# Two-layer decoder trunk: one pass of 512 columns for both words of the tokens in half of the first expert product, with the modulation loads moved to the second product

## The chip, the cores and the metric

The kernel runs on one core of one Trainium2 chip. The metric is the device time of one execution in microseconds (us). Engines are named as in the profile: PE is TensorE (its weight loads are PEld), DVE is VectorE, ACT is ScalarE, POOL is GpSimd, and SP is the queue that issues the DMAs.

## The reference, cut to what matters

Two residual layers work on 256 tokens of 1024 features. Each layer has a mixer (convolution and forgetting attention in layer 0, sparse attention in layer 1) and then an expert mixer, `peer_ffn`, which this change is about:

```python
def chunk(xc):
    q = (xc @ w_q).reshape(-1, PEER_HEADS, 2, half)
    s = jnp.einsum('thpd,pkd->thpk', q, sub_keys)
    sv, si = lax.top_k(s, PEER_TOPK)
    cand = (sv[:, :, 0, :, None] + sv[:, :, 1, None, :])...
    cv, ci = lax.top_k(cand, PEER_TOPK)
    ...
    g = jax.nn.softmax(cv, axis=-1)
    a = jax.nn.gelu(jnp.einsum('td,thkd->thk', xc, ue))
    return jnp.einsum('thk,thkd->td', (g * a), ve)
```

There are 16384 experts, each one row of `peer_u` and one of `peer_v`. Each layer also scales, shifts and gates its input by six vectors that come out of `silu(c) @ ada_w`.

## The kernel before, in words

The experts are not gathered. The kernel multiplies all of `peer_u` with all tokens, block by block of 128 experts (128 blocks, `j`, each one load of 128 x 1024 floats), puts the gelu of the products into `S`, multiplies `S` by the gate of each token and expert (zero for most), and multiplies that with `peer_v`, again 128 loads.

Every float32 operand is written as a sum of two words: `hi`, rounded by ACT (line L83), and `lo`, the rest, which DVE subtracts (L84). A product is three matmuls, hi·hi, hi·lo and lo·hi (`terms`, issued by `contract`, L105). Loaded words rotate through 5 buffers (`raw`), 3 of `hi` and 3 of `lo`. A `raw` buffer comes free when its `lo` is made, and only then does SP issue the load that takes its place.

One call of `peer` goes through these stages:

1. `score` and `choose`: the query product (`pwq`, `psc`) and the search for the best experts on DVE. `choose` is a generator: its pieces are taken two at a time while the first half of the blocks is multiplied.
2. First half of `mm1`: blocks 0 to 63, in pairs, into one PSUM bank (512 columns) for a pair. The stationary operand is a 128 x 128 piece of the expert word, the moving one 256 tokens, with 8 pieces `k` for a block. At its end `weigh` turns the chosen indices (`pT` on PE, then DVE).
3. Second half of `mm1`: 32 steps of `gating` (`pG`) and one pair of blocks each.
4. `mm2`: 64 pairs of `peer_v` blocks into `y`; here the tokens are stationary and 512 columns of the expert word move.

The modulation vectors need 48 loads of `ada_w` for each layer; each is reduced by one DVE instruction (L157), which waits for its load. Those that stage 1 of the program has not done are handed to `peer(0, early, late)`: `early` has 39 entries (38 loads) and `late` 18 loads. Before, 20 of the early ones go beside the pairs from block 24 on in stage 2, and 19 entries beside the first 32 pairs of `mm2`. `beside` issues a load behind one pair and its reduction behind the next. A load takes a `raw` buffer like an expert block.

The order of each engine's instructions is made by a scheduler at build time from the program and is then fixed: every engine, and SP, runs its list in order, and an instruction that waits holds all behind it. PSUM has eight banks; in `peer` they are `a` (2, the products), `b` (2, `pT` and the sums of squares) and `w` (2 double banks, `psc`, `pG`, `y`).

Of the kernel before, what the change touches and what calls it, by code (L numbers as in the profile page):

```python
# [8 lines left out]
F32R = mybir.dt.float32r  # L9
F16 = mybir.dt.float16  # L10
U32 = mybir.dt.uint32
AF = mybir.ActivationFunctionType
ALU = mybir.AluOpType
# [4 lines left out]
P = 128  # L18
D = 1024
KC = 8  # L20
T = 256
# [31 lines left out]
def trunk(ctx: ExitStack, tc: tile.TileContext, xT, c, ada_w, ada_b, norm_g, even_w, even_wf, even_bf,  # L53
# [3 lines left out]
    V, A, G, PE = nc.vector, nc.scalar, nc.gpsimd, nc.tensor  # L57
# [1 line left out]
    cp = ctx.enter_context(tc.tile_pool(name="const", bufs=1))  # L59
    st = ctx.enter_context(tc.tile_pool(name="stream", bufs=2))  # L60
    ps = [None]
    MIX, PEER = dict(a=2, b=3, y=3), dict(a=2, b=2, w=2)

    def banks(sizes):
        if ps[0] is not None:
# [9 lines left out]
    def load(src):  # L75
        t = st.tile([P, D], F32, tag="raw", bufs=RAW, name="raw")
        nc.sync.dma_start(t, src)
        return t

    def split(raw):  # L80
        hi = st.tile([P, D], F32R, tag="hi", bufs=HI, name="hi")
        lo = st.tile([P, D], F32R, tag="lo", bufs=HI, name="lo")
        A.activation(hi, raw, AF.Copy)  # L83
        V.tensor_tensor(lo, raw, hi.bitcast(F32), op=ALU.subtract)  # L84
        return Op(None, hi, lo)
# [3 lines left out]
    def weights(src):  # L89
        w = split(load(src))  # L90
        if meanwhile[0] is not None:
            meanwhile[0]()
        return w

    def bank(tag, name):
        pool, sizes = ps[0]
        return pool.tile([P, 512], F32, tag=tag, bufs=sizes[tag], name=name)

    def wide_bank(name):
# [3 lines left out]
    def contract(dst, pairs, start=True, stop=True, **kw):  # L103
        for n, (a, b) in enumerate(pairs):
            PE.matmul(dst, a, b, start=start and n == 0, stop=stop and n == len(pairs) - 1, **kw)  # L105

    def over_d(w, x, k0=0, k1=KC, order=(0, 1, 2)):

        return [t for k in range(k0, k1)
                for t in map(terms(w.at(lambda a: a[:, k * P:(k + 1) * P]), x.at(lambda a: a[:, k, :])).__getitem__, order)]  # L110


    def exps():

        tc.keep_in_program_order(A.preload_act_table_set("natural_log_exp_and_others"))
# [584 lines left out]

    def peer(l, early, late, after=None):
        pp = tc.alloc_tile_pool(name="peer", bufs=1, reuse_waits="tile")
        hi, lo = (pp.tile([P, KC, T], F32R, name=f"h_{n}") for n in ("hi", "lo"))
        s0 = tc.alloc_tile_pool(name="s0", bufs=1, side="right", reuse_waits="tile")
        S = [s0.tile([P, 64, T], F32, name="S0"), pp.tile([P, 64, T], F32, name="S1")]
        if True:
# [128 lines left out]
            gated = [0]  # L835

            def mm1(j):


                p = bank("a", "pmm1")  # L840
                for s in range(2):
                    contract(p[:, s * T:(s + 1) * T], over_d(weights(peer_u[l, j + s]), h))
                p = p.rearrange("p (a t) -> p a t", a=2)
                s = S[j // 64][:, j % 64:j % 64 + 2]
                n = gated[0]
                if n < T:
                    A.activation(s[:, :, n:], p[:, :, n:], AF.Gelu_apprx_tanh)  # L847
                if n > 0:
                    A.activation(p[:, :, :n], p[:, :, :n], AF.Gelu_apprx_tanh)
                    V.tensor_tensor(s[:, :, :n], s[:, :, :n], p[:, :, :n], op=ALU.mult)  # L850
# [77 lines left out]
            def spread(fs, n):  # L928

                return [fs[len(fs) * i // n:len(fs) * (i + 1) // n] for i in range(n)]  # L930
# [18 lines left out]
            if l == 0:  # L949
                pinned(rows, bass.AP(tensor=bdr.tensor, offset=bdr.offset, ap=[[0, P], [1, 16 * NB]]))  # L950
            start = 24
            lots = spread(early[:20], (64 - start) // 2)
            for j in range(0, 64, 2):
                mm1(j)
                for _ in range(2):
# [6 lines left out]
                gating(64 + 2 * b)  # L962
                mm1(64 + 2 * b)
            exps()
            for b, fs in enumerate(spread(early[20:], 32)):
                mm2(2 * b)
                beside(fs)
            s0.release()
# [140 lines left out]
```

## Time and profile before

| | us |
|---|---|
| median of 3 runs | 1948.03 (1946.95 to 1949.16) |
| profiled execution, its own time | 1949.57 |
| its span, first to last instruction | 1947.5 |
| layer 0: first half of `mm1`, second half with gating | 187.5, 214.7 |
| layer 0: `mm2`, first and second 32 pairs | 181.0, 177.7 |
| layer 1: first half of `mm1`, second half with gating | 188.0, 214.8 |
| layer 1: `mm2`, first and second 32 pairs | 173.9, 174.1 |

The stages are cut at the first instruction of the next one on PE. The same stage stands in both layers, with the `ada_w` loads in layer 0 alone, so that layer 1 shows what a stage takes without them.

### The profile page before, as it was taken

The numbers are of one execution on the slowest core, as the hardware profiler recorded it, in microseconds if no ns is written. First come the engines' busy times: TensorE is split into PE (matmuls) and PEld (weight loads), VectorE is DVE, ScalarE is ACT, GpSimd is POOL, SyncE is SP. The second block draws the span as 40 slices with busy tenths as digits, with TensorE's granted clock in tenths as the row PEclk, the third lists the DMA queues.
The fourth block names the chain that finished last, engine by engine and source line by source line (L and its number), as shares of the span: only waits on it lengthen the run. The fifth ranks groups of instructions, "written<-read, shape, count | busy, mean of one in ns | idle before, by whom it ended". The sixth has DMA issues, their size and how long they took to land.

```text
span 1947.5 us, 33150 instructions
## 1 busy us (share of the span) xinstructions
PE 1888.0 (97%) x12954; PEld 1695.0 (87%) x12954; DVE 1439.3 (74%) x2918; ACT 929.7 (48%) x1359; POOL 3.6 (0%) x13
## 2 busy tenths in 40 slices
PE   4898999999999999999999989999999999999998
PEld 3788999999999877877788679999999998888887
DVE  7776999788998666666656859994888985555554
ACT  4445444444445444444445654454444454444443
POOL 0000000000000000000000000000000000000000
PEclk8899999999999999999989999999999999999999
DMA  8865568854446777877633124655444456655563
GB/s 308 272 217 195 175 210 262 279 165 160 156 154 219 237 242 260 295 240 252 230 116 104 45 93 153 193 185 183 160 159 152 162 190 192 193 195 194 195 195 119
DMA packets 105591, 375.00 MB, mean 193 GB/s; under 512 B 12715, under 2 KB 16860, under 8 KB 104540
## 3 DMA queue, kind: packets, MB, share of 16 engines
q1 hardware_dynamic: 104860, 372.38, 58.0%
q8 instruction: 101, 1.65, 0.4%
q10 hardware_dynamic: 576, 0.52, 0.1%
q14 instruction: 54, 0.44, 0.1%
HBM read 369.16 MB, written 6.31 MB: 193 GB/s over the span
## 4 chain that ended last, share of the span: by engine, by line
PE 51%; issue 41%; DVE 4%; DMA 2%; ACT 1%; SPq 0%; DVEq 0%; POOL 0%; POOLq 0%; ACTq 0%
PE y L105 18%; PE pmm L105 18%; PE po L105 2%; PE pG L105 1%; PE pq L105 1%; PE pcc L105 1%; DVE lo L84 1%; DMA raw<-in_ada_w_dram 1%; PE s L650 1%; PE pv L105 1%; PE pt L354 1%; PE po_att L665 1%; DMA S<-in_keys_dram 1%; PE pm L183 1%; PE pb L105 1%
## 5 line engine op out<-in xcount | busy, mean ns | idle before, releaser
L83 ACT ACTIVATE hi<-raw 128x1024 fp32r<-128x1024 f32 x588 | 620.6, 1056 | 696.1 <-PE pmm L105 409.8
L84 DVE TENSOR_TENSOR lo<-raw,hi 128x1024 fp32r<-128x1024 f32 x588 | 717.1, 1223 | 186.3 <-ACT hi L83 185.9
L105 PE MATMUL pmm<-h_hi,hi 128*128 128x256 f32 x2048 | 584.4, 286 | 0.0
L105 PE MATMUL pmm<-h_lo,hi 128*128 128x256 f32 x2048 | 578.7, 283 | 0.0
L105 PE MATMUL pmm<-h_hi,lo 128*128 128x256 f32 x2048 | 577.9, 283 | 0.1
L105 PE MATMUL y<-lo,h_hi 128*128 128x512 f32 x1024 | 399.8, 390 | 6.5 <-DVE lo L84 6.5
L105 PE MATMUL y<-hi,h_lo 128*128 128x512 f32 x1024 | 398.2, 389 | 0.0
L105 PEld LDWEIGHTS pmm<-h_hi,hi 128*128 128x128 f32 x2048 | 392.5, 192 | 0.2
L105 PEld LDWEIGHTS pmm<-h_lo,hi 128*128 128x128 f32 x2048 | 392.6, 192 | 0.0
L105 PEld LDWEIGHTS pmm<-h_hi,lo 128*128 128x128 f32 x2048 | 391.7, 192 | 0.6 <-DVE lo L84 0.3
L105 PE MATMUL y<-hi,h_hi 128*128 128x512 f32 x1024 | 357.7, 389 | 0.0
L105 PEld LDWEIGHTS y<-lo,h_hi 128*128 128x128 f32 x1024 | 192.2, 188 | 51.1 <-DVE lo L84 11.4
L105 PEld LDWEIGHTS y<-hi,h_hi 128*128 128x128 f32 x1024 | 192.1, 188 | 40.3 <-ACT hi L83 0.4
L105 PEld LDWEIGHTS y<-hi,h_lo 128*128 128x128 f32 x1024 | 192.2, 188 | 39.6
L157 DVE CUSTOM_DVE_ANT_0 raw<-raw,silu 128x1024 f32<-128x1024 f32 x96 | 117.3, 1224 | 131.4 <-DMA raw<-in_ada_w_dram 131.1
L894 ACT ACTIVATE h_hi<-S 128x512 fp32r<-128x512 f32 x128 | 80.7, 632 | 177.9 <-PE y L105 177.7
L895 DVE TENSOR_TENSOR h_lo<-S,h_hi 128x512 fp32r<-128x512 f32 x128 | 88.1, 691 | 60.4 <-ACT h_hi L894 60.4
L870 DVE TENSOR_TENSOR w<-hot 128x1024 f16<-128x1024 f16 x128 | 88.1, 689 | 45.3 <-PE pG L105 45.3
L866 DVE TENSOR_TENSOR hot<-hot,lane 128x1024 f16<-128x1024 f16 x128 | 87.7, 686 | 0.0
L880 DVE TENSOR_TENSOR S<-S,pG 128x512 f32<-128x512 f32 (+31 forms) x126 | 69.3, 550 | 1.7 <-PE pG L105 1.7
L105 PE MATMUL pG<-w,hot 128*128 128x128 f16 x1024 | 68.4, 220 | 0.0
L847 ACT ACTIVATE S<-pmm 128x512 f32<-128x512 f32 (+31 forms) x126 | 59.9, 476 | 0.0
(273 smaller groups left out, 1873.1 us busy)
## 6 DMA issues: line engine op xcount, KB each, us to landing
raw<-in_peer_u_dram SPq DMA_DIRECT2D x256, 512.0 KB, 3.4
raw<-in_peer_v_dram SPq DMA_DIRECT2D x256, 512.0 KB, 3.6
raw<-in_ada_w_dram SPq DMA_DIRECT2D x96, 512.0 KB, 4.7
raw<-in_even_w_dram SPq DMA_DIRECT2D x24, 512.0 KB, 4.5
raw<-in_odd_w_dram SPq DMA_DIRECT2D x20, 512.0 KB, 4.0
raw<-in_w_q_dram SPq DMA_DIRECT2D x16, 512.0 KB, 3.8
raw<-in_even_wo_dram SPq DMA_DIRECT2D x8, 512.0 KB, 3.4
raw<-in_odd_wo_dram SPq DMA_DIRECT2D x8, 512.0 KB, 3.3
```

Source lines behind the costliest of these rows:

```text
L83: A.activation(hi, raw, AF.Copy)
L84: V.tensor_tensor(lo, raw, hi.bitcast(F32), op=ALU.subtract)
L105: PE.matmul(dst, a, b, start=start and n == 0, stop=stop and n == len(pairs) - 1, **kw)
L157: V.tensor_tensor_reduce(out=w, in0=w, in1=silu, op0=ALU.mult, op1=ALU.add, scale=1.0, scalar=0.0, accum_out=mods[:, l, m:m + 1])
L183: PE.matmul(pm[0], mean_d.to_broadcast([P, P]), sq, start=(k == 0), stop=(k == KC - 1))
L354: PE.transpose(pt[:, n * P:(n + 1) * P], p[:, n * P:(n + 1) * P], ident)
L847: A.activation(s[:, :, n:], p[:, :, n:], AF.Gelu_apprx_tanh)
L866: V.tensor_tensor(pairs(x), words(v), pairs(lane[:, None].to_broadcast([P, UNIT, P])), op=ALU.is_equal)
L870: V.tensor_tensor(pairs(x), pairs(o), words(g), op=ALU.mult)
L880: V.tensor_tensor(s[:, :n], s[:, :n], p[:, 64 * f:64 * f + n], op=ALU.mult)
L894: A.activation(x.hi, s, AF.Copy)
L895: V.tensor_tensor(x.lo, s, x.hi.bitcast(F32), op=ALU.subtract)
```

## The change

- For blocks 0 to 63 the two token words stand beside each other (`both`, k by word by token). The hi piece of the expert word streams both, 512 columns, in one matmul; the lo piece streams the hi tokens, 256 columns, into the second half of the same bank. A block has 16 matmuls in place of 24.
- A block now fills a bank: 256 columns of hi·hi and 256 of the two others. ACT copies the second half to `S`, DVE adds the first half to it (a new instruction for each block), and the gelu goes from `S` to `S` for a pair.
- The banks become `a` (4) and `w` (2); what asked for `b` in `peer` now takes an `a`.
- All 39 early entries go beside the first 32 pairs of `mm2`, none beside `mm1`.

```diff
-    MIX, PEER = dict(a=2, b=3, y=3), dict(a=2, b=2, w=2)
+    MIX, PEER = dict(a=2, b=3, y=3), dict(a=4, w=2)
...
     def bank(tag, name):
         pool, sizes = ps[0]
+        tag = tag if tag in sizes else "a"
         return pool.tile([P, 512], F32, tag=tag, bufs=sizes[tag], name=name)
...
-        hi, lo = (pp.tile([P, KC, T], F32R, name=f"h_{n}") for n in ("hi", "lo"))
+        both = pp.tile([P, KC, 2, T], F32R, name="h_both")
+        hi, lo = both[:, :, 0], both[:, :, 1]
...
             def mm1(j):
+                if gated[0] == 0:
+                    t = S[j // 64][:, j % 64:j % 64 + 2]
+                    for s in range(2):
+                        w, p = weights(peer_u[l, j + s]), bank("a", "pmm1")
+                        for k in range(KC):
+                            a, b = (x[:, k * P:(k + 1) * P] for x in (w.hi, w.lo))
+                            PE.matmul(p, a, both[:, k].rearrange("p u t -> p (u t)"), start=(k == 0),
+                                      stop=(k == KC - 1), skip_group_check=True)
+                            PE.matmul(p[:, T:], b, hi[:, k], start=False, stop=(k == KC - 1), skip_group_check=True)
+                        A.activation(t[:, s], p[:, T:], AF.Copy)
+                        V.tensor_tensor(t[:, s], t[:, s], p[:, :T], op=ALU.add)
+                    A.activation(t, t, AF.Gelu_apprx_tanh)
+                    return
                 p = bank("a", "pmm1")
...
-            lots = spread(early[:20], (64 - start) // 2)
+            lots = spread([], (64 - start) // 2)
...
-            for b, fs in enumerate(spread(early[20:], 32)):
+            for b, fs in enumerate(spread(early, 32)):
                 mm2(2 * b)
                 beside(fs)
```

The change moves instructions in two places that matter below. The first is the list of SP in `mm2` of layer 0, from the third pair on; `in_peer_v_dram` is an expert block, `in_ada_w_dram` a modulation load. Before:

```order
L77 DMA raw<-in_peer_v_dram 128x1024 x4
L77 DMA raw<-in_ada_w_dram 128x1024
L77 DMA raw<-in_peer_v_dram 128x1024 x4
L77 DMA raw<-in_ada_w_dram 128x1024
L77 DMA raw<-in_peer_v_dram 128x1024 x2
L77 DMA raw<-in_ada_w_dram 128x1024
L77 DMA raw<-in_peer_v_dram 128x1024 x4
```

The same place of SP's list in the changed kernel:

```order
L77 DMA raw<-in_peer_v_dram 128x1024 x2
L77 DMA raw<-in_ada_w_dram 128x1024
L77 DMA raw<-in_peer_v_dram 128x1024 x2
L77 DMA raw<-in_ada_w_dram 128x1024
L77 DMA raw<-in_peer_v_dram 128x1024 x2
L77 DMA raw<-in_ada_w_dram 128x1024 x2
L77 DMA raw<-in_peer_v_dram 128x1024 x2
```

Before, most modulation loads have four expert blocks between them; over the first 64 blocks the list has 18 of them, and 5 times only two blocks (one pair) stand between two. Now it has 36 over these 64 blocks, 28 times with one pair between two, and 6 times two in a row.

The second place is the list of DVE at the end of the first half of `mm1` in layer 0, where the chosen indices come back from PE in `pT`. `hot`, `gr` and `w` are made for the gates, `lo` for the next blocks. Before:

```order
L828 CAST hot<-pT 128x512 x2
L84 TENSOR_TENSOR lo<-raw,hi 128x1024
L866 TENSOR_TENSOR hot<-hot,lane 128x1024 x2
L830 TENSOR_SCALAR gr<-pT 128x256
L84 TENSOR_TENSOR lo<-raw,hi 128x1024
L831 CAST hot<-gr 128x512
```

In the changed kernel L852 is the new addition, with the number of the bank that it reads:

```order
L84 TENSOR_TENSOR lo<-raw,hi 128x1024
L852 TENSOR_TENSOR S_1600<-S_1600,pmm_3744 128x256
L830 CAST hot<-pT 128x512 x2
L832 TENSOR_SCALAR gr<-pT 128x256
L881 TENSOR_TENSOR hot<-hot,lane 128x1024
L84 TENSOR_TENSOR lo<-raw,hi 128x1024
L852 TENSOR_TENSOR S_1600<-S_1600,pmm_3769 128x256
```

PE's list has the block of `pmm_3769`, then the six transposes into three `pT` banks, then the block of `pmm_3820`. Before, `pT` had banks of its own; now `pmm_3769`, three `pT` and `pmm_3820` take the four `a` banks in turn, and the last of them takes the bank that the addition of `pmm_3769` empties.

## Rows read from the trace of the kernel before

**Rows 1.** The page: span, and busy time, share and instructions of each engine.

```profile
span 1947.5 us, 33150 instructions
PE 1888.0 (97%) x12954; PEld 1695.0 (87%) x12954; DVE 1439.3 (74%) x2918; ACT 929.7 (48%) x1359; POOL 3.6 (0%) x13
```

**Rows 2.** Busy time by stage: `mm1` halves of layers 0 and 1, then `mm2`.

```profile
core 0: us, PE busy (x) PEld busy (x) DVE busy (x) ACT busy (x) POOL busy (x), PEclk, DMA share, GB/s
209.45:396.98 187.53, 187.53 (x1576) 186.98 (x1575) 173.10 (x533) 87.55 (x100) 0.00 (x0) 1.00 0.72 234
1188.49:1376.47 187.98, 187.88 (x1576) 187.07 (x1575) 153.43 (x495) 87.60 (x100) 0.00 (x0) 1.00 0.56 182
396.98:611.66 214.68, 214.68 (x2050) 213.30 (x2049) 190.10 (x283) 100.77 (x162) 0.00 (x0) 1.00 0.49 161
...
611.66:792.61 180.95, 176.65 (x770) 143.41 (x769) 119.53 (x142) 86.60 (x100) 0.00 (x0) 1.00 0.77 257
...
1591.25:1765.19 173.94, 173.94 (x768) 143.99 (x768) 102.31 (x99) 86.30 (x99) 0.00 (x0) 1.00 0.60 196
```

**Rows 3.** The chain that ended last, layer 1: start, length, what, how many.

```profile
1224.96 139.51 PE pmm L105 x1161
...
1377.54 5.80 PE pmm L105 x48
...
1591.25 348.21 PE y L105 x1536
```

**Rows 4.** Busy time in layer 1 until the choice of experts is done.

```profile
1188.49:1303.00 114.51, 114.41 (x964) 113.65 (x963) 113.06 (x449) 54.38 (x62) 0.00 (x0) 1.00 0.57 183
```

**Rows 5.** Waits in that stretch: who waited for whom, total us, times, longest.

```profile
PEld pmm L105 <- DVE lo L84: 0.3, 1, 0.3
```

**Rows 6.** Groups by shape in layer 0's gating: 256 columns read from PSUM.

```profile
L880 DVE TENSOR_TENSOR S<-S,pG 128x256 f32<-128x256 f32 x1 | 0.4, 414 | 0.0
...
L882 ACT ACTIVATE S<-pG 128x256 f32<-128x256 f32 x1 | 0.4, 383 | 0.1
```

**Rows 7.** Timeline of DVE in layer 1, around the return of the chosen indices.

```profile
1364.72 1.29 DVE L828 CAST hot<-pT 128x512 f16<-128x512 f32 x2 [0.90 <-PE pT L826]
1365.93 0.68 DVE L866 TENSOR_TENSOR hot<-hot,lane 128x1024 f16<-128x1024 f16 x1
1366.53 1.22 DVE L84 TENSOR_TENSOR lo<-raw,hi 128x1024 fp32r<-128x1024 f32 x1
1367.66 0.69 DVE L866 TENSOR_TENSOR hot<-hot,lane 128x1024 f16<-128x1024 f16 x1
1368.27 0.42 DVE L830 TENSOR_SCALAR gr<-pT 128x256 f32<-128x256 f32 x1
```

**Rows 8.** Waits from 611 to 790 us, nearly the first 32 pairs.

```profile
DVE raw L157 <- DMA raw<-in_ada_w_dram: 49.2, 17, 4.0
...
PEld y L105 <- DVE lo L84: 7.6, 8, 1.4
```

**Rows 9.** Timeline of DVE there, two modulation loads with one pair between.

```profile
660.98 1.23 DVE L157 CUSTOM_DVE_ANT_0 raw<-raw,silu 128x1024 f32<-128x1024 f32 x1 [2.79 <-DMA raw<-in_ada_w_dram]
...
662.13 1.22 DVE L84 TENSOR_TENSOR lo<-raw,hi 128x1024 fp32r<-128x1024 f32 x1
663.27 0.68 DVE L895 TENSOR_TENSOR h_lo<-S,h_hi 128x512 fp32r<-128x512 f32 x1
663.88 1.22 DVE L84 TENSOR_TENSOR lo<-raw,hi 128x1024 fp32r<-128x1024 f32 x1
667.86 1.23 DVE L157 CUSTOM_DVE_ANT_0 raw<-raw,silu 128x1024 f32<-128x1024 f32 x1 [2.77 <-DMA raw<-in_ada_w_dram]
...
669.01 1.22 DVE L84 TENSOR_TENSOR lo<-raw,hi 128x1024 fp32r<-128x1024 f32 x1
```

**Rows 10.** Timeline of PE at the end of that stretch.

```profile
670.29 0.50 PE L105 MATMUL y<-lo,h_hi 128*128 128x512 f32 x1 [0.69 <-DVE lo L84]
```

**Rows 11.** Timeline of SP there: the issue of the second load.

```profile
663.38 0.33 SPq L77 DMA_DIRECT2D raw<-in_ada_w_dram  x1
```

## The prediction

> **What bounds the kernel now.** Start with the page: PE is busy 1888.0 of 1947.5 us [rows 1], so a gain has to come out of PE's list, and a loss is a gap in it. The table by stage is next, because the two layers run the same expert stages, and only layer 0 has modulation loads in them. In the first half of `mm1` PE has no gap in layer 0 and 0.1 us in layer 1, with the granted clock at 1.00 [rows 2]. In `mm2` the first 32 pairs take 180.95 us in layer 0, with 4.30 us of PE idle, and 173.94 us in layer 1, with none [rows 2]. What differs is the `ada_w` loads: 7.01 us.
>
> The chain gives the pace of PE where it waits for nothing: 139.51 us for 1161 matmuls of 256 columns (120.2 ns each) in `mm1`, 5.80 us for 48 (120.8) between gates, and 348.21 us for 1536 of 512 columns (226.7) in `mm2` [rows 3]. Twice the columns cost 106.5 ns more, and 13.7 ns are left over for each matmul whatever its length. Each has its own weight load.
>
> **PE's part of the change.** For one `k` the old list has three matmuls of 256 columns, 3 x 120.2 = 360.6 ns; the new one has one of 512 and one of 256, 226.7 + 120.2 = 346.9 ns. It streams the same 768 columns and saves the left-over of one matmul, 13.7 ns. There are 64 blocks x 8 = 512 of these in a layer: 7.0 us per layer, 14.0 us in all. Below, nothing is saved if the left-over goes with columns and not with matmuls; more than 14.0 I see no row for.
>
> The Trainium skill, "TensorE: Matmul & The Clock Gate", section "Back-to-back issue gap", gives a gap of N/2.4 + 2.5 ns at full clock, and its Part 2 says that the engine pulls a weight load ahead of running matmuls. By that the saving would be 1024 x 2.5 = 2.6 us. The rows of this case have 13.7 where the page has 2.5, at both lengths, so I go by the rows.
>
> **What the new join costs.** Each block adds on ACT a copy of 128x256 out of PSUM, 383 ns in the nearest row, and on DVE an addition of 128x256 with one operand in PSUM, 414 ns; the gelu stays one instruction for a pair [rows 6]. ACT is busy 87.6 of 188 us there [rows 2]; 64 x 0.38 = 25 us more leaves it slack. DVE has none to spare at first: in layer 1 it is busy 113.06 of the first 114.51 us, until the experts are chosen [rows 4], and it fell so far back that PE once waited for a `lo`, 0.3 us [rows 5]. Over the whole half it is busy 153.43 us [rows 2]; with 64 x 0.41 = 26 us it comes to 180, and the half should shrink to 188.0 - 7.0 = 181. Back to back, an instruction begins before the one ahead has ended (a `lo` of 1.22 us lets the next begin after 1.14 [rows 9]), which leaves a few us. So the sum just fits, and the lists spread the choice over more blocks than before. I take 1.5 us of waiting for late `lo` words in a layer; 0 if the lists keep pace, 7 us if all of PE's gain is lost to DVE.
>
> Layer 0 loses its modulation loads from this half. That gains nothing by itself, since PE did not wait there [rows 2]; it makes the room for the additions on DVE, 19 x 1.23 = 23 us [rows 9] against 26.
>
> **The shared banks.** With `b` gone, the three `pT` take `a` banks, and the next block needs the bank that the addition of `pmm_3769` frees. That addition stands on DVE behind two casts, `gr`, `hot` and a `lo`, all of which begin after `pT`. From the timeline, start to start: two casts 1.21, `hot` 0.60, a `lo` 1.13 [rows 7]; then `gr` and the addition, 0.42 [rows 7] and 0.41 [rows 6]: 3.8 us in which PE has nothing in its list that it may begin. Before, `pT` had banks of its own and PE went on. I take 3.8 us per layer; below 0 if the bank comes free otherwise, above 5 with a wait for the copy on ACT.
>
> Together each layer's first half gains 7.0 - 1.5 - 3.8 = 1.7 us: 3.4 us in all (from a gain of 14 to a loss of 10). The second half of `mm1` keeps its instructions and its 214.7 us [rows 2].
>
> **The moved loads.** What a modulation load does in `mm2` is seen in rows 8 to 11. DVE waits 49.2 us for such loads, 17 times [rows 8]. Why it waits shows in the timeline. DVE reduces a load at 660.98, makes a `lo` at 662.13, which ends at 663.35 and sets a `raw` buffer free; at 663.38 SP issues the next modulation load into it [rows 9, 11]. DVE makes one more `lo` and then stands before the reduction until 667.86, 4.5 us after the issue, with the next `lo` behind it [rows 9]. That one begins at 669.01, and PE, which needs it, goes on at 670.29 after a gap [rows 9, 10]. From reduction to reduction this is 667.86 - 660.98 = 6.88 us, while PE wants a pair in 24 x 0.2267 = 5.44 us. A pair with such a turn around costs 1.44 us, and the next one as much, because the loop feeds itself.
>
> With four blocks between two loads the loop has two pairs of time, 10.9 us, and costs nothing. That fits the whole: five places with one pair between two loads in the old list, and 7.01 us more than layer 1: 1.40 us each. It is a delay and no lack of rate: DMA is 0.77 busy at 257 GB/s [rows 2], and the same engines had 0.72 in `mm1` of layer 0.
>
> The new list has 28 such places over these pairs, and six times two loads in a row. The first two I let the lead of the three `hi` and `lo` buffers absorb: 26 x 1.40 = 36.4 us, less the 7.0 that are there now: 29.4 us more. The second load of a doubled pair is not in any row. Below it is free, as both wait in the same 4.5 us; above it adds a turn of its own and its reduction, 6 x (1.44 + 1.15) = 15.5 us. I take nothing for it. For the whole term: below -7 (if all come in time, as they did in `mm1`, where a pair took 5.8 us and DVE interleaved them with other work), above 29.4 + 15.5 = 45.
>
> **Sum.** -3.4 + 29.4 = +26 us on the span of 1947.5, and as much on the executions: the profiled one took 1949.57 with 2.1 us around its span, the median of the runs is 1948.03. Forecast: 1948.0 + 26 = 1974 us, 1.3% slower.
>
> **Rivals.**
> *The loads hide.* The list puts a reduction behind both `lo` of a pair, and if DVE does other work while the load comes, the loop takes less than 5.44 us and the 29.4 fall away. For it: in `mm1` of layer 0 twelve pairs in a row had a load each, and PE never waited [rows 2]. Against it: those pairs were 5.8 us long and DVE had the choice of experts to do in between; in `mm2` it has 2.9 us of work for a pair and stands still for the rest [rows 9]. Then the time is 1948 - 3.4 - 7 = 1938, or 1931 with the banks free too. It decides below about 0.4 us per such place: 26 x 0.4 = 7.0 + 3.4. Faster.
> *DVE falls behind in `mm1`.* Both halves lose PE's gain and the banks cost 5 us: 14.0 - 2 x (7 + 5) = -10, so 1948 + 10 + 29.4 = 1987. For it, [rows 4, 5]; against it, the sum over the whole half, which fits.
> *The weight load is hidden.* If the left-over does not go with the matmul, PE gains nothing, but DVE keeps pace too: 1948 + 29.4 + 2 x 3.8 = 1985. For it: only that no row has the two lengths in turn; against it, the same 13.7 ns at 256 and 512 columns [rows 3]. The gap of the Trainium skill named above ("TensorE: Matmul & The Clock Gate", "Back-to-back issue gap") would make it 1982.
> *Half the loads hide*, in the first pairs and after each gap: 14 x 1.40 - 7.0 - 3.4 = +9, 1957.
>
> **How the numbers follow.** The forecast has 0.56, DVE falling behind 0.12, the hidden weight load 0.06, half of the loads hiding 0.13, and all of them hiding 0.13. The predicted time is the first case's, 1974. The range of 8 in 10 runs from 1953 (below it the loads that hide and a little of the half case) to 1990 (above it the doubled loads at their full price): about 0.14 and 0.06 are left out. A measurement of this kernel tells 0.2%, 4 us, from no change. Faster than 1944 is the case of hidden loads, 0.11; within 4 us its near side, 0.05; slower holds 0.84.
>
> **What would show it.** In the changed profile: 512-column `pmm` matmuls at 226.7 ns and 256 ones at 120.2; one gap of 3 to 4 us on PE behind `pT` in each layer; first halves of `mm1` at 185 to 187 us; the first 32 pairs of layer 0's `mm2` at 210 us with some 30 us of PE idle ended by `lo`, and DVE waiting for `ada_w` loads some 35 times; the other stages as now. Wrong would be a stretch of `mm2` near 181 us, or `mm1` halves near 181 or above 190, or a granted clock below 1.00 in the stretch with the gaps, which the gaps of now do not show [rows 2].

## The result, and the profile after

The changed kernel takes 1960.07 us (median of 5 runs, 1957.81 to 1961.44), the kernel before 1948.02 (5 runs, 1946.95 to 1949.16). The ratio is 1.0052, with a 95% interval of 1.0039 to 1.0065: 12 us slower, where 26 were forecast. The time lies inside the range.

The page of the changed kernel has the same two rows as [rows 1]. PE has 1024 matmuls fewer and 5 us less to do, on a span that is 12.2 us longer:

```profile
span 1959.7 us, 31492 instructions
PE 1883.0 (96%) x11930; PEld 1638.1 (84%) x11930; DVE 1479.9 (76%) x3046; ACT 967.9 (49%) x1487; POOL 3.6 (0%) x13
```

The table by stage answers to [rows 2]: first halves of `mm1` in layers 0 and 1, then the first 32 pairs of `mm2` in layer 0.

```profile
core 0: us, PE busy (x) PEld busy (x) DVE busy (x) ACT busy (x) POOL busy (x), PEclk, DMA share, GB/s
211.04:395.91 184.87, 184.22 (x1064) 159.35 (x1063) 172.12 (x556) 106.30 (x163) 0.00 (x0) 1.00 0.58 183
...
610.52:810.28 199.76, 183.84 (x770) 144.71 (x769) 138.54 (x179) 86.08 (x99) 0.00 (x0) 0.98 0.83 281
...
1202.59:1388.58 185.99, 184.77 (x1065) 159.40 (x1063) 173.13 (x557) 106.30 (x163) 0.00 (x0) 1.00 0.58 184
```

Stage by stage, cut at the first instruction of each on PE:

| stage | before | after | forecast | measured |
|---|---|---|---|---|
| up to the first `pmm` | 209.45 | 211.04 | 0 | +1.6 |
| first half of `mm1`, layer 0 | 187.53 | 184.87 | -1.7 | -2.7 |
| first half of `mm1`, layer 1 | 187.98 | 185.99 | -1.7 | -2.0 |
| `mm2`, layer 0, first 32 pairs | 180.95 | 199.76 | +29.4 | +18.8 |
| its second 32 pairs, to the first `pkc` | 195.39 | 192.97 | 0 | -2.4 |
| `pkc` to layer 1's first `pmm` | 200.49 | 199.34 | 0 | -1.2 |

The other stages are within 0.1 us. The rows add up to +12.1. The +1.6, -2.4 and -1.2 were not forecast. They lie in code that the diff does not touch; behind `y`, at least, its PE list has another order (`pyT` and the sums of squares stand otherwise between the `pbias` matmuls). From `y` to `pkc` alone the kernels below take 14.0 to 21.7 us, so nothing is built on it.

The waits of the stretch with the loss answer to [rows 8]:

```profile
DVE raw L158 <- DMA raw<-in_ada_w_dram: 53.2, 32, 3.3
...
PEld y L106 <- DVE lo L84: 22.7, 22, 2.7
PE y L106 <- DVE lo L84: 13.6, 11, 2.3
ACT hi L83 <- DMA raw<-in_peer_v_dram: 11.5, 4, 6.6
```

DVE waits 32 times for a modulation load, nearly the 35 of the forecast, but 1.7 us each in place of 2.9. Three pieces of that stretch show how unequal the pairs are: four pairs with one load each, then one pair behind two loads in a row, and the last two pairs.

```profile
696.22:719.11 22.89, 22.85 (x97) 17.71 (x96) 15.61 (x20) 10.59 (x13) 0.00 (x0) 1.00 0.84 275
719.11:728.39 9.28, 7.33 (x25) 5.59 (x24) 7.79 (x10) 2.75 (x4) 0.00 (x0) 0.82 0.84 280
794.02:810.28 16.26, 13.36 (x49) 9.95 (x48) 8.54 (x12) 4.33 (x6) 0.00 (x0) 0.90 0.94 349
```

A single load costs 22.89 / 4 - 5.44 = 0.28 us; the pair behind the doubled one costs 3.84. Half of that is the clock (PE is busy for 7.33 us in place of 5.44): behind a gap of 1.95 us on PE the granted clock is 0.50 from 721.8 to 725.1, the lower of its two levels (1.2 in place of 2.4 GHz), and 0.82 in the mean of the piece, where every stage of [rows 2] has 1.00. A gap of 2.30 us, which ended at 777.21, left it at 1.00.

In the last two pairs, at the turn to the second 32 and 5.4 us over the pace, the constants of the next mixer come through the same queue. The DMA engines are 0.94 busy there, ACT waits 11.4 us for expert words, and DVE stands before the scaling of one of the constants; DVE and then PE:

```profile
801.33 0.15 DVE L528 TENSOR_SCALAR og<-og 128x1 f32<-128x1 f32 x1 [4.80 <-DMA og<-in_odd_g_dram]
...
802.30 0.73 PE L106 MATMUL y<-hi,h_both 128*128 128x512 f32 x2 [2.15 <-ACT hi L83]
```

From pair to pair, start to start on PE, the 25.7 us over 32 x 5.44 divide so: 17.2 in the ten pairs at and behind six doubled loads (1.3 to 3.8 for each doubling), 5.4 in the last two, where a seventh doubling stands too, and 3.1 in the 20 others.

### The profile page after: what moved, and what is told of

It is laid out like the page before. It is cut to its first block, busy times and chain, and to the rows that moved or that the text cites. A ratio compares the mean times of both kernels' runs of the same rounds, so it can differ in the third digit from the quotient of the medians.

```text
span 1959.7 us, 31492 instructions
## 1 busy us (share of the span) xinstructions
PE 1883.0 (96%) x11930; PEld 1638.1 (84%) x11930; DVE 1479.9 (76%) x3046; ACT 967.9 (49%) x1487; POOL 3.6 (0%) x13
## 4 chain that ended last, share of the span: by engine, by line
PE 51%; issue 42%; DVE 3%; DMA 3%; ACT 1%; DVEq 0%; POOL 0%; POOLq 0%; ACTq 0%
PE y L106 18%; PE pmm L106 9%; PE pmm L848 6%; PE pmm L850 3%; PE po L106 2%; DMA raw<-in_ada_w_dram 1%; PE pG L106 1%; PE pq L106 1%; PE pwq L106 1%; PE pcc L106 1%; PE s L651 1%; DVE lo L84 1%; PE pt L355 1%; DMA S<-in_keys_dram 1%; PE po_att L666 1%
## 5 line engine op out<-in xcount | busy, mean ns | idle before, releaser
L106 PE MATMUL y<-hi,h_both 128*128 128x512 f32 x2048 | 633.9, 390 | 2.2 <-ACT hi L83 2.2
L106 PEld LDWEIGHTS y<-hi,h_both 128*128 128x128 f32 x2048 | 385.8, 188 | 82.3 <-ACT hi L83 2.6
L106 PE MATMUL y<-lo,h_both 128*128 128x512 f32 x1024 | 403.2, 394 | 16.0 <-DVE lo L84 15.6
L106 PE MATMUL pmm<-h_both,hi 128*128 128x256 f32 x2048 | 375.8, 285 | 0.0
L848 PE MATMUL pmm<-h_both,hi 128*128 128x512 f32 x1024 | 361.7, 398 | 0.7 <-DVE hot L830 0.7
L106 PEld LDWEIGHTS pmm<-h_both,hi 128*128 128x128 f32 x2048 | 318.1, 191 | 0.0
L850 PE MATMUL pmm<-h_both,lo 128*128 128x256 f32 x1024 | 288.3, 282 | 1.2 <-DVE lo L84 1.1
L106 PE MATMUL pmm<-h_both,lo 128*128 128x256 f32 x1024 | 289.2, 282 | 0.0
L106 PEld LDWEIGHTS y<-lo,h_both 128*128 128x128 f32 x1024 | 193.2, 189 | 67.1 <-DVE lo L84 27.6
L848 PEld LDWEIGHTS pmm<-h_both,hi 128*128 128x128 f32 x1024 | 192.3, 188 | 47.8 <-DVE hot L830 1.2
L106 PEld LDWEIGHTS pmm<-h_both,lo 128*128 128x128 f32 x1024 | 195.9, 191 | 0.0
L850 PEld LDWEIGHTS pmm<-h_both,lo 128*128 128x128 f32 x1024 | 193.4, 189 | 2.9 <-DVE lo L84 2.4
L910 DVE TENSOR_TENSOR h_both<-S,h_both 128x512 fp32r<-128x512 f32 x128 | 88.0, 690 | 56.1 <-ACT h_both L909 56.1
```

Source lines behind the costliest of these rows:

```text
L848: PE.matmul(p, a, both[:, k].rearrange("p u t -> p (u t)"), start=(k == 0), stop=(k == KC - 1), skip_group_check=True)
L850: PE.matmul(p[:, T:], b, hi[:, k], start=False, stop=(k == KC - 1), skip_group_check=True)
L910: V.tensor_tensor(x.lo, s, x.hi.bitcast(F32), op=ALU.subtract)
```

## The experiments

The theory after the result: the moved loads alone make the loss of 18.8 us, by the loop through the raw buffers, at another price than forecast. The rival: the join, which gives DVE and the scheduler another order, or the DMA rate makes it.

**Which part of the change.** One kernel has the moved loads alone, the other the join and the banks alone:

```diff
 loads_only, from the kernel before
-            lots = spread(early[:20], (64 - start) // 2)
+            lots = spread([], (64 - start) // 2)
-            for b, fs in enumerate(spread(early[20:], 32)):
+            for b, fs in enumerate(spread(early, 32)):
 join_only, from the changed kernel: these two lines the other way round
```

> The kernel before, with the one edit that all early modulation loads go beside the first 32 pairs of the second product; the join and the banks stay as they were. Theory: the loads take raw buffers there whatever the first product does, so the first 32 pairs of layer 0 go from 181 to 199 us, both first halves of the first product stay at 187.5 and 188.0, and the time is 1948 + 18 = 1966 us. Rival: the loads cost so much only with the new order of DVE that the join makes, and alone they are nearly hidden: that stretch stays below 185, 1950 us.

Measured: 1964.89 us, ratio 1.0067 (1.0051 to 1.0084). The first 32 pairs take 200.24 us, and `mm1` in layer 0 stays at 187.52 although DVE lost 19 reductions there (152.5 us busy in place of the 173.1 of [rows 2]). So the loads alone make the loss, as the theory has it, and leaving `mm1` gains nothing.

> The changed kernel with the modulation loads back where they were (20 beside the first product, 19 beside the second). Theory: the first 32 pairs of the second product go back from 199.8 to 181 us, and the first half of the first product in layer 0 has no room on DVE: 172 us busy now and 19 reductions of 1.15 us more are 194 us, so it grows from 184.9 to about 195; 1960 - 19 + 10 = 1951 us. Rival: DVE takes the reductions in its gaps and hands what is left to the stage behind, the half stays at 185: 1941 us, and the move of the loads was not needed at all.

Measured: 1957.75 us, ratio 1.0037 (1.0025 to 1.005). The windows of the first half of `mm1` in layer 0, the half with gating, and the first 32 pairs:

```profile
209.94:406.41 196.47, 183.91 (x1049) 158.19 (x1048) 192.37 (x594) 105.39 (x161) 0.00 (x0) 0.97 0.68 222
406.41:623.65 217.24, 217.24 (x2065) 215.50 (x2064) 191.77 (x285) 102.74 (x166) 0.00 (x0) 1.00 0.50 161
623.65:804.53 180.88, 177.11 (x771) 143.32 (x769) 119.48 (x142) 86.60 (x100) 0.00 (x0) 1.00 0.77 258
```

DVE is busy 192.37 of 196.47 us, and the waits have one of 11.0 us of `pT` for the last step of the choice: with the additions, the reductions have no room beside `mm1`, as the prediction's sum of DVE said. The stages are those of the theory, the time is not (1951 was expected). So the loss has two forms: 11.6 us in `mm1` where the loads stay, 18.8 in `mm2` where they go.

**What the stall is.** In `own_space` the loads of the first 32 pairs no longer take raw buffers; the order changes along with the buffers, since each reduction now comes ahead of the issue of the next load:

```diff
-    def ada(l, m, later=False):
+    def ada(l, m, later=False, own=None):
-        w = load(ada_w[l, m])
+        w = load(ada_w[l, m]) if own is None else own
+        if own is not None:
+            nc.sync.dma_start(w, ada_w[l, m])
...
+                if own:
+                    for f in waiting:
+                        f()
+                    waiting[:] = []
+                begun = [f(hot[0][:, 2 * n:2 * n + 2].rearrange("p a b -> p (a b)").bitcast(F32) if own else None)
+                         for n, f in enumerate(fs)]
```

> The changed kernel; the modulation loads beside the first 32 pairs of the second product go into the 8 KB of a partition that the gates have left free by then (two places of 4 KB), and no longer into the raw buffers of the expert blocks. Same loads, same bytes, same reductions. Theory: the 18.8 us are the loop through the raw buffers (a buffer comes free late, its load comes 4 to 5 us later, and everything on DVE stands behind the reduction); with places of their own the loads are asked for earlier and the first 32 pairs fall from 199.8 to 174 to 179 us: 1935 to 1939 us. Rival: 16 DMA engines that are 0.83 busy are the limit and the loads come as late as now: the stretch stays above 192, 1952 us or more.

Measured: 1947.08 us, 0.9986 (0.9975 to 0.9997). The stretch falls by 19.7 us to 180.10, nearly what the theory has, with the DMA engines at 0.89 and 301 GB/s: over the stretch rate is not the limit, the raw buffers are. DVE still waits there for such loads, 28 times and 37.0 us, and PE loses little by it. The sum gains 13 us and not 19.7; the stages around it give the rest back.

The next kernel takes away the doubled loads alone:

```diff
-            for b, fs in enumerate(spread(early, 32)):
+            for b, fs in enumerate(spread(early[:32], 32)):
-            for b, fs in enumerate(spread(late, 32)):
+            for b, fs in enumerate(spread(early[32:] + late, 32)):
```

> The changed kernel, but no pair of blocks in the second product has more than one modulation load beside it: 32 entries beside the first 32 pairs, the other seven are put ahead of the late ones, beside the second 32 pairs (25 loads there, one at a time). Theory: a place with one pair between two loads costs 0.3 us and not 1.40, and what costs is the load that comes doubled, 2 to 3 us each; the first 32 pairs fall from 199.8 to about 185 us and the second 32 grow by 2: 1948 us. Rival: every load costs the same, 18.8 us over 20 loads; moving seven takes 6 us from the first half and gives 6 to the second, 1960 us.

Measured: 1978.91 us, 1.0133 (1.0107 to 1.0159), 19 us slower than the changed kernel, and neither expectation. The first 32 pairs take 192.89 us, but the second 32, with seven loads more, 197.86 in place of 178.35. Single loads have two prices; here are four pairs and three pairs, each with one load beside it.

```profile
741.29:764.66 23.37, 22.96 (x97) 17.71 (x96) 16.82 (x21) 10.59 (x13) 0.00 (x0) 1.00 0.86 272
936.76:957.74 20.98, 17.24 (x73) 13.28 (x72) 13.06 (x16) 7.92 (x10) 0.00 (x0) 1.00 0.66 218
```

DVE and SP's queue in the first, 5.84 us a pair (the first column is the start):

```profile
744.96 1.23 DVE L158 CUSTOM_DVE_ANT_0 raw<-raw,silu 128x1024 f32<-128x1024 f32 x1 [1.63 <-DMA raw<-in_ada_w_dram]
...
746.11 0.69 DVE L910 TENSOR_TENSOR h_both<-S,h_both 128x512 fp32r<-128x512 f32 x1
746.71 2.35 DVE L84 TENSOR_TENSOR lo<-raw,hi 128x1024 fp32r<-128x1024 f32 x2
750.76 1.22 DVE L158 CUSTOM_DVE_ANT_0 raw<-raw,silu 128x1024 f32<-128x1024 f32 x1 [1.70 <-DMA raw<-in_ada_w_dram]
...
746.22 0.33 SPq L77 DMA_DIRECT2D raw<-in_ada_w_dram  x1
```

and in the second, 6.99 us a pair:

```profile
938.97 1.23 DVE L158 CUSTOM_DVE_ANT_0 raw<-raw,silu 128x1024 f32<-128x1024 f32 x1 [3.38 <-DMA raw<-in_ada_w_dram]
...
940.12 1.22 DVE L84 TENSOR_TENSOR lo<-raw,hi 128x1024 fp32r<-128x1024 f32 x1
...
945.92 1.23 DVE L158 CUSTOM_DVE_ANT_0 raw<-raw,silu 128x1024 f32<-128x1024 f32 x1 [2.84 <-DMA raw<-in_ada_w_dram]
...
941.37 0.33 SPq L77 DMA_DIRECT2D raw<-in_ada_w_dram  x1
```

The load at 746.22 starts when the reduction itself has ended (744.96 + 1.23 = 746.19): it takes the buffer that the reduction emptied. From reduction to reduction pass 1.26 + 4.54 = 5.80 us, 0.36 above the pace. The load at 941.37 starts when the first `lo` behind the reduction has ended (941.34): 1.15 + 1.22 + 0.03 + 4.55 = 6.95 us, 1.5 above. The second is the loop of [rows 9, 11], which the forecast took for all places. In the changed kernel 25 of the 36 loads of this stretch start 0.04 us behind the end of a reduction; six of the others are second loads of a doubled pair and start behind a `lo`.

If so, the order of DVE should set the price. In both kernels of the next pair DVE's list is held to an order over the first 32 pairs of the kernel `singles`:

```diff
 forced_hll, from singles
+            with tc.manual_schedule(engines={mybir.EngineType.DVE}) if l == 0 else ExitStack():
                 for b, fs in enumerate(spread(early[:32], 32)):
 forced_lhl: so too, and the first word of mm2 is split ahead of the tokens
+                first = weights(peer_v[l, j])
                 A.activation(x.hi, s, AF.Copy)
...
```

> The kernel with one modulation load for each pair (32 entries beside the first 32 pairs), and DVE kept in the order of the program over these pairs of layer 0: the rest of the tokens, both lo, the reduction. Theory: in this order the modulation load takes the buffer that the reduction itself has emptied, so from reduction to reduction pass 1.15 us of reduction and 4.65 of load, 5.80 against a pace of 5.44; the first 32 pairs take 174 + 31 x 0.36 = 185 us. Rival: the order has no part in it and the stretch stays at the 193 us that it takes with the order of the scheduler.

> As the run with the kept order, but DVE goes lo, rest of the tokens, lo, reduction. Theory: now the load waits for the buffer of the first lo behind the reduction; 1.15 + 1.14 + 4.65 = 6.95 us from reduction to reduction, 1.5 us above the pace for each of 31 pairs, and the first 32 pairs take 174 + 47 = 220 us, 35 more than with the other order for the same instructions and the same bytes. Rival: DVE and DMA have the same work in both, and both stretches are within 5 us of each other.

Measured: the stretch takes 174.47 and 174.11 us, in both the pace of layer 1 without any load (medians 1965.52 and 1958.62; the second 32 pairs, not held, take 206.6 and 201.3). Both theories fall, and so does a price that goes by the order of `lo` and reduction; the rival of the second, that the two come out alike, holds. What the price goes by shows in the rows of `forced_hll`, DVE and then SP:

```profile
691.38 1.23 DVE L84 TENSOR_TENSOR lo<-raw,hi 128x1024 fp32r<-128x1024 f32 x1 [1.10 <-ACT hi L83]
692.52 1.22 DVE L158 CUSTOM_DVE_ANT_0 raw<-raw,silu 128x1024 f32<-128x1024 f32 x1
...
697.96 1.22 DVE L158 CUSTOM_DVE_ANT_0 raw<-raw,silu 128x1024 f32<-128x1024 f32 x1
...
692.63 0.33 SPq L77 DMA_DIRECT2D raw<-in_ada_w_dram  x1
```

The list of DVE repeats the same four steps as at 744.96, but here the load takes the buffer of the `lo` that ended ahead of the reduction, at 692.61. It has 5.33 us until the next reduction and takes 4.8 in the median; in the whole stretch DVE waits once for such a load, 0.8 us. The reduction is no longer a link of the loop. So the price of a single load fits the instruction that has emptied the buffer which it takes, and that comes out of the lists of SP and DVE together: the `lo` ahead of the reduction 0, the reduction 0.36, the `lo` behind it 1.5 us where such pairs follow each other. This is read from the rows; no run moves one of the two lists and holds the other.

Three more kernels try that account: the changed kernel with the `with` line of `forced_hll` (`kept_all`), the kernel before with the same line (`kept_before`), and `forced_hll` with each reduction one pair earlier (`kept_early`; `s0_open` is set over the first 32 pairs):

```diff
                 begun = [f() for f in fs]
+                if l == 0 and s0_open[0]:
+                    for f in begun:
+                        f()
+                    return
```

> The changed kernel, all 39 early entries beside the first 32 pairs as it has them (six times two loads in a row), but DVE kept in the order of the program over these pairs of layer 0. Theory: the 18.8 us come from where the list of DVE puts the reductions; behind both lo of the next pair a reduction finds its load there and the next load takes a buffer that a lo has emptied before it. The first 32 pairs take 174 to 178 us and the time is 1960 - 23 = 1937 us. Rival: the doubled loads need buffers, which are short, whatever the order: 174 + 6 x 2.5 = 189 us or more.

Measured: 1960.43 us, 1.0055 (1.0036 to 1.0075): the rival. The stretch takes 195.10 us, and the waits have moved:

```profile
ACT hi L83 <- DMA raw<-in_peer_v_dram: 73.2, 47, 4.3
DVE lo L84 <- ACT hi L83: 44.5, 43, 3.1
```

One reduction still waits, for 1.0 us, but expert words come late. 8.5 of the 21 us over the pace are lost in the last pair, beside the constants:

```profile
790.45:804.39 13.94, 5.92 (x25) 4.24 (x23) 6.40 (x14) 2.29 (x3) 0.00 (x0) 0.89 1.01 368
```

The other 12.5 lie nearly all in the pairs at and behind the six doublings. With one load for a pair the raw buffers suffice (174.47), with the doubled ones they don't: the changed kernel's 18.8 us are not the place of the reductions alone.

> The kernel before with one edit: DVE is kept in the order of the program over the first 32 pairs of the second product in layer 0 (19 entries there, as it has them). Theory: the 7 us that these pairs take above layer 1 have the same cause, reductions that stand too early; they fall from 181 to 174 us, 1948 - 7 = 1941 us. Rival: with loads two pairs apart the order has no part in it: 180 us, 1947.

Measured: 1946.02 us, 0.998 (0.9967 to 0.9993). The stretch falls from 180.95 to 174.47, as expected, and the time is the rival's. The second 32 pairs take 182.90 in place of 177.70 and give most of it back, in the pair at the turn (11.41). So of the 7 us that the forecast took off, the part before the turn, 4.8 us by pairs, has this cause. The rest the kernel before loses beside the constants, and at the turn a loss remains. Two pieces of the kernel before: a pair at one of the five places that the forecast priced, 1.0 us over the pace, and the last three pairs, 2.1 us over it:

```profile
666.26:672.72 6.46, 5.77 (x25) 4.43 (x24) 4.86 (x6) 2.65 (x4) 0.00 (x0) 1.00 0.66 226
774.20:792.61 18.41, 17.17 (x73) 13.28 (x72) 11.90 (x15) 8.04 (x10) 0.00 (x0) 1.00 1.02 373
```

> One load for each of the first 32 pairs and the order of DVE kept, as in the run that took 174 us there, but each load is reduced at the end of the pair beside which it is asked for, one pair earlier. The buffers are the same. Theory: the reduction now stands before its load has landed, with the next pair's words behind it: each of the 31 pairs takes at least 1.4 us more, 218 us or more for the 32 pairs. Rival: the place of the reduction has no part in it: 174 to 178 us.

Measured: 174.49 us in the stretch (1957.15 in all), the rival, but the run doesn't tell the two apart: SP's list moved along, each load now starts 7.75 us ahead of its reduction. An earlier try, `reduce_later`, with each reduction a pair later in the program (`waiting` holds two pairs' loads), left DVE's list as it was, instruction for instruction as the trace names them, so that its 1961.57 us only repeat the changed kernel.

> The changed kernel, but each modulation load of the second product is reduced two pairs after it is asked for, where it was one. Theory: raw buffers are what is short; a buffer is held a pair longer, of five two are with modulation loads, and what DVE no longer waits for them ACT waits for expert words: the first 32 pairs stay above 192 us, 1953 us or more. Rival: what costs is that DVE stands before the reduction with the next lo behind it; a pair later the load is there, and the stretch falls to 181 to 186 us: 1942 to 1947 us.

**The pace of the two lengths.**

```diff
                         for k in range(KC):
-                            a, b = (x[:, k * P:(k + 1) * P] for x in (w.hi, w.lo))
+                            a = w.hi[:, k * P:(k + 1) * P]
...
+                        for k in range(KC):
+                            b = w.lo[:, k * P:(k + 1) * P]
```

> The changed kernel; a block of the first half does its eight matmuls of 512 columns first and its eight of 256 behind them, where they took turns. Theory: the 6.7 ns that a pair of 512 and 256 takes above 226.7 + 120.2 belong to the change of length, of which one in eight is left; a k then takes 347.7 ns and not 353.6, 3 us in each layer, and the word lo is wanted later, which takes away most of the PE waits for it (1 us in each layer): 1960 - 8 = 1952 us. Rival: the 6.7 ns belong to the weight load or to the accumulation of each matmul and stay: the pace stays at 353.6 and the time within 2 us of 1960.

Measured: 1959.39 us, 1.0038 (1.0024 to 1.0052); both first halves of `mm1` take 182.63 us, 2.2 and 3.4 less. The stages come near the theory, the time is the rival's. From the start of block 26 to that of block 58 are 256 `k`. In groups of eight they take 349.2 ns each:

```profile
287.06:376.45 89.39, 89.39 (x515) 78.67 (x514) 82.87 (x260) 54.82 (x85) 0.00 (x0) 1.00 0.61 195
```

In turn they have two paces. The same blocks in layers 0 and 1 of `kept_all`, whose `mm1` is that of the changed kernel, take 346.7 and 353.3 ns a `k`:

```profile
287.80:376.55 88.75, 88.75 (x515) 78.25 (x513) 80.96 (x247) 54.39 (x84) 0.00 (x0) 1.00 0.60 196
1281.04:1371.49 90.45, 90.45 (x515) 78.39 (x513) 81.17 (x246) 54.05 (x84) 0.00 (x0) 1.00 0.58 193
```

The first is the 346.9 of the forecast, so the change of length by itself costs nothing, and the theory of this run falls although its stages came out nearly as it has them. The changed kernel goes at 347 in blocks 2 to 7 of both layers and at 353 from block 11 on. The pace changes at a few blocks alone (10, 24 or 60), often where PE has just waited some tenths of a us; what decides between the two stays open. A block of `hi_then_lo` on PE:

```profile
1230.96 2.00 PE L848 MATMUL pmm<-h_both,hi 128*128 128x512 f32 x8
1232.80 1.12 PE L852 MATMUL pmm<-h_both,lo 128*128 128x256 f32 x8
1233.75 2.00 PE L848 MATMUL pmm<-h_both,hi 128*128 128x512 f32 x8
```

Start to start, eight of 512 take 1.84 us, 230 ns each against the 226.7 of [rows 3]. Why these are dearer wasn't settled. In the sum, most of the gain is lost to the rest of the program (16.46 us between `y` and `pkc`, 1.8 more, and 0.8 to 1.4 in each of three other stages).

**What the join is worth where the loads cost nothing.** `before_own` is the kernel before with all early loads in `mm2` in places of their own; `best` is the changed kernel with the grouped matmuls, one load for a pair at most, and places of their own in both halves of `mm2`; `best_three` has the loads of `best` and the products and banks of the kernel before; `kept_best` is `best` with the loads in raw buffers and DVE's list held over all 64 pairs by the line above, and with the scaling of `og` later in the program. The lines of `best` that place the loads:

```diff
-            for b, fs in enumerate(spread(early, 32)):
+            for b, fs in enumerate([[]] + spread(early[:31], 31)):
...
-                beside(fs)
+                beside(fs, lambda: hot[0])
...
+                ad = tc.alloc_tile_pool(name="ad", bufs=1, side="right", reuse_waits="tile")
+                room = ad.tile([P, 4, 1024], F16, name="room")
-            for b, fs in enumerate(spread(late, 32)):
+            for b, fs in enumerate(spread(early[31:] + late, 32)):
...
-                beside(fs)
+                beside(fs, lambda: room)
```

> The kernel before (three matmuls of 256 columns, banks as they were) with all early modulation loads beside the first 32 pairs of the second product and in two places of their own, in the 8 KB that the gates have left free. It differs from the changed kernel with the same places only by the join and the banks. Theory: the join is worth what the two first halves of the first product showed, 2 to 5 us: halves 187.5 and 188.0, first 32 pairs at 180, 1950 us against 1947. Rival: the join gains nothing in the sum, since the stages around give it back: 1947 us here too.

Measured: 1946.51 us, 0.9977 (0.9965 to 0.999). Against the 1947.08 of `own_space`, which ran on another chip, the join's 4 us in `mm1` (187.75 and 187.98 against 185.69 and 186.10) are gone again in the first 32 pairs (176.37 against 180.10): the rival.

> The changed kernel with the 512-column matmuls of a block ahead of its 256-column ones, all modulation loads of the second product one for each pair at most and in two places of their own (31 in the first 32 pairs, from the second on, in the 8 KB that the gates leave; the rest beside the second 32 pairs, in room that the first half of the gated products leaves). Theory: with no raw buffer taken the second product runs near the 174 us that it takes without loads in layer 1, 175 to 177 us in each half; first halves of the first product 182.7: 1960 - 23 - 2 - 5 = 1930 us, faster than both kernels. Rival: 57 loads more than layer 1 has cost their DMA time (0.89 busy where they have places of their own), the halves stay at 180: 1941 us.

Measured: 1933.59 us, 0.9915 (0.9888 to 0.9942), and 1932.54, 0.9898 (0.988 to 0.9916), in a second set of runs on another chip: the theory, within 4 us. The windows of that second one, `mm1` in layer 0 and the two halves of `mm2`:

```profile
210.66:393.30 182.64, 182.29 (x1065) 159.88 (x1063) 171.78 (x554) 107.43 (x164) 0.00 (x0) 1.00 0.59 185
607.98:783.85 175.87, 174.44 (x770) 144.12 (x769) 135.81 (x169) 85.69 (x99) 0.00 (x0) 1.00 0.85 300
783.85:959.81 175.96, 174.84 (x770) 143.94 (x768) 125.73 (x148) 84.38 (x95) 0.00 (x0) 1.00 0.78 270
```

> The kernel before (three matmuls of 256 columns, no join, banks as they were) with the modulation loads as in the fastest kernel so far: in places of their own, one for each pair at most. Theory: with nothing left to give back, the join is worth what its stages show, 187.6 against 182.6 us in each first half of the first product: 10 us more than the fastest, 1943 us. Rival: the order of the second product changes as well and gives half of it back, as it did between the two kernels with own places in the first 32 pairs alone: 1938 us or less.

Measured, on the same chip as that second set: 1939.81 us, 0.9938 (0.992 to 0.9956). The join, in groups of eight, is worth 10.3 us in `mm1` (187.76 and 187.77 against 182.64 and 182.63), and 7 in the sum, between the two expectations.

> The changed kernel with the 512-column matmuls of a block ahead of its 256-column ones, one modulation load for a pair at most (32 entries beside the first 32 pairs, 26 beside the second) in the raw buffers as ever, and DVE kept in the order of the program over all 64 pairs of layer 0. Theory: places of their own aren't needed: 174.5 us in the first 32 pairs and 175 to 178 in the second, 1930 us, level with the fastest so far. Rival: in the second half the constants of the next mixer come through the same queue and a DVE that may not pass over a late load stands still: 185 us there, 1940 us.

Measured: 1936.62 us, 0.9937 (0.9916 to 0.9958). This lies between the two expectations. Raw buffers do for single loads: 174.47 and 180.24 us, of the latter 6 in the one pair at the turn from one half to the other (11.43). DVE's list has the scaling of `og` there all the same, ahead of a `lo`:

```profile
789.44 0.15 DVE L531 TENSOR_SCALAR og<-og 128x1 f32<-128x1 f32 x1 [7.81 <-DMA og<-in_odd_g_dram]
```

## Why the prediction was wrong

**The sign and the place were right, the size was not.** The term that failed is "28 places with one pair between, 26 x 1.40 - 7.0 = +29.4"; it measured +18.8. Its mechanism, a loop of buffer, load and reduction, is there, but its length was read at one place of the old list [rows 9, 11], where the load takes the buffer of a `lo` behind the reduction, and carried over to all. In the new list most loads take the reduction's own buffer, and a pair with one such load costs 0.28 us. The rows for it were at hand: the lists of SP and DVE show what stands ahead of each load, and the pace is 5.44.

**The check by the five old places fitted by luck.** The 7.01 us divided by five gave 1.40, next to the loop's 1.44. But the pair of rows 9 to 11 takes 6.46 us on PE, 1.0 over the pace, three more take 6.44, 6.65 and 6.25, and the first 5.61. That is 4.2 us for the five; 2.1 of the rest stand in the last three pairs, beside the constants of the next mixer.

**The doubled loads were the other half of the mistake.** The forecast took nothing for them, with a bound of 2.59 us each; they cost 17.2 us with the pairs behind them, 2.9 each, clock and all. `kept_all` shows the shortage of buffers that they make. So in place of the 36.4 of the forecast the single loads have 3.1, the doubled ones 17.2, and the last two pairs 5.4, of which it isn't shown how much the moved loads make. That the time still lies inside the range is due to these errors going opposite ways. The granted clock of the stretch is 0.98, which the forecast had named as a sign of being wrong.

**The PE term was half there.** 7.0 us a layer were forecast; PE's busy time in the halves fell by 3.3 and 3.1 [rows 2]. The slower of the two paces, 353.3 ns a `k`, holds for most of both halves and saves 7 ns of 360.6 in place of 13.7, and what decides for it is open. That the 13.7 are the same at both lengths was no check by the rows alone, which have two numbers for two unknowns. The Trainium skill's gap ("TensorE: Matmul & The Clock Gate", "Back-to-back issue gap"), which that section gives for a single matmul by itself and not for a stream with weight loads, would have given an estimate of 2.6 us in all; the 6.4 measured lie between that and the 14.0 of the forecast.

**The shared banks cost a tenth of their term.** PE goes on 0.35 us behind `pT`, and not 3.8:

```profile
383.76 0.38 PE L828 MATMUL pT<-ident,S 128*128 128x128 f32 x2
384.49 0.50 PE L848 MATMUL pmm<-h_both,hi 128*128 128x512 f32 x1 [0.35 <-DVE hot L830]
```

It waited for the cast of the first `pT`, not for the addition of the block ahead, which DVE began at 387.02: the bank that it took was the first one to come free, and not the next in turn. That was the lower bound.

**DVE in `mm1` kept pace, as forecast:** busy 172.12 and 173.13 us, where 180 were worked out; PE is idle for 0.65 and 1.22, of which 0.3 and 0.9 are waits for a `lo`, where 1.5 were put in. The addition took 411 to 413 ns and the copy 364, where 414 and 383 were put in. That `mm1` came near the forecast, -4.7 against -3.4, is luck too: PE's gain was put too high and the banks too dear.

**The rivals.** DVE falling behind in `mm1` did not come, but `join_only` shows that it was 19 reductions away. "Half the loads hide", 1957, came nearest in the number; not half were hidden, nearly all single ones were cheap and the doubled ones dear.

## What to carry to other kernels

Price a load in a loop by the instruction that empties the buffer it takes, at each place of the new list, and not by a mean price per place: here the same load cost 0, 0.3 or 1.0 to 1.5 us, and 1.3 to 3.8 where two came in a row. Work without a due date that goes into a stage with a tight loop should have a buffer of its own: here 8 KB a partition that lay idle took 13 us off the changed kernel's time. With such places in both halves, one load a pair at most, and the change of order on PE, the loss of 12 us became a gain of 18 to 19. What one stage gains can be given back by lists that a scheduler makes anew elsewhere; read the sum stage by stage, and a stage pair by pair before a mean price is taken from it.

## What the runs showed of the hardware

Matmuls of 512 and 256 columns in turn have two paces at a granted clock of 1.00: 346.7 ns a pair, the sum of what each length takes among its own kind [rows 3], or 353.3; in groups of eight they take 349.2. Behind a gap of 1.95 us on PE the granted clock fell to 1.2 GHz (mean 0.82 over 9.28 us), and behind one of 2.30 us it did not. Modulation loads beside expert loads, at 300 GB/s and a DMA share of 0.85, still came in time when they had a buffer early enough; at the turn, where the share was 0.94 to 1.02, expert words came late.
